# Products of b and k with the decayed rows over 64 rows, two heads side by side, and a new order of TensorE's pieces

## The chip, the cores and the metric

The kernel runs on one core of a Trainium2 chip. The metric is the device time of one execution in microseconds, median of several runs. A core has TensorE (PE in the profile: matmuls; PEld: its weight loads), VectorE (DVE), ScalarE (ACT), GpSimd (POOL) and SyncE (SP, which issues most of the DMAs here). Each engine works through its own queue in order and waits on semaphores.

## The reference, cut to what matters

Two layers of a transformer trunk for 512 latent and 128 context tokens. Each layer has three groups of heads side by side: windowed attention, full attention, and a recurrent mixer (RWKV-7 time mixing) with 6 heads of 64, run in both directions over the tokens. Only the mixer is touched. It is this scan, for each head and direction:

```
def wkv_step(S, inp):
    r, w, k, v, a, b = inp
    sa = jnp.einsum('bhvk,bhk->bhv', S, a)
    S = S * w[:, :, None, :] + sa[..., None] * b[:, :, None, :] + v[..., None] * k[:, :, None, :]
    y = jnp.einsum('bhvk,bhk->bhv', S, r)
    return S, y
...
xs = tuple(jnp.moveaxis(t, 1, 0) for t in (rh, heads(decay), kt, vh, -kk, kk * ah))
S_fin, y = lax.scan(wkv_step, init_state[:, d].astype(f32), xs, reverse=(d == 1))
```

## The kernel before, in words

All arithmetic here is in fp32, for which TensorE issues two matmul instructions for one product; the counts below are instructions as the profile shows them.

The mixer works on tiles of 128 tokens in five groups; a group is a pair of tiles, one for each direction d (the list `groups` pairs tile 0 with 3, 1 with 2, the context tile 4 with itself, 2 with 1, 3 with 0). A tile has two chunks cc of 64 tokens. The 6 heads lie as three pairs pr; in a pair, head e = 0 has partitions 0 to 63 and head e = 1 partitions 64 to 127 (`HS[e]`). A group goes through these generators:

- `front(g)`, L1039, in 15 pieces. For each direction: decay and gate projections (L1045, L1048); tanh (L1050, the one after it on VectorE L1051); the triangle sum of the log decays (L1063); exponentials; then the rows of b and k (buffer `BK`) divided by the running decay, and `W`, which holds the rows of a (columns 0 to 63) and r (64 to 127) times the running decay. `W[HS[e], e]` is written by GpSimd and VectorE (L1083, L1084); the other half, `W[HS[1-e], e]`, is cleared by GpSimd (L1082). After that, for each direction, chunk and head, the products of `BK` with `W` (L1102): four pieces for a direction, each of three products of 128 rows by 128 columns into one bank of PSUM, in which the cleared half of `W` cuts out the other head's rows. Each result is drained from PSUM by one copy on ScalarE (L1105) and two masked operations on VectorE (L1106, L1109); L1109 writes the half of `W` that was cleared. Then come 24 matmuls L1119, after which the triangles go to DRAM, and `relay(g)`. The last two pieces transpose `BK` (L1135) into `TK`: six transposes for a head into one bank, copied by ScalarE (L1137).
- `relay(g)`, L1142: 16-by-16 diagonal blocks come back from DRAM and GpSimd inverts them in 30 small operations (L1150, L1152). VectorE makes a transposed copy (L1154), and both go to DRAM again (L1156).
- `solve(g)`, L1159: loads these blocks (L1164) and inverts the whole triangles in four iterations for both directions (24 matmuls L1172 each, then VectorE L1183 or L1193).
- `rec(g)`, L1286: the recurrent steps of four chunks, each in three pieces (L1216 and L1219; L1226; L1234 and L1237), chained over the state.

Beside them run `fm_tail` (the last input projections), `bonus` and `finalize` (normalisation of the mixer's output), `tail_memory` (loads of the output weights) and `out_part` (the output projection, L1439).

The order of TensorE's instructions is written by hand: inside `tc.manual_schedule(engines={PE})` (L1442) `weave` takes one piece after another from these generators, in the order of the letters of `WEAVE` (L39): a, b, g, j, m are the fronts of groups 0 to 4; d, f, i, l, o their solves; e, h, k, n, p their recs; c the value and state transposes; q `fm_tail`; r `tail_memory`; s, t, u output projection; v to y bonus and finalize. The order on the other engines is made by the framework at compile time. The pieces of `front`, of `bonus` and of `finalize` share a ring of two PSUM banks, `pf` (L953); `BK` has two slots, `W` six, the exponentials one (`PeR`).

Of the kernel before, what the change touches and what calls it, by code (L numbers as in the profile page):

```python
# [35 lines left out]
TYPS, HELD = (1, 0), 3  # L36
MODW, BES = 512, 1
TS = (0, 1, 2, 3, 4), (0, 1, 2, 3, 4)
WEAVE = ("aqqaaqaqaqqaqqqaaqqaqaqqqaqaaqqqqqqqqqcacbbabccccbbcbccdbbbddbcbbcdbdbdgdcdbdggeggeegfgfgeggfggefgeeeeeeefggffjjjhffijjhjjjhjjhhiijhjhihhhjhhjmmjikimiimimkmklmmkklmmlmkmmlkkkklkkllnrmllmnvvnnorronovnnonnwvnnvnoorrpvrowowoppwpwsswssspwpswspwpsppswppwttwttxttwtsyutxttuuytxuttttuuuyuuuuuuuu",  # L39
         "aqqaaqaqaqqaqqqaaqqaqaqqqaqaaqqqqqqqqqcacbbabccccbbcbccdbbbddbcbbcdbdbdgdcdbdggeggeegfgfgeggfggefgeeeeeeefggffjjjhffijjhjjjhjjhhiijhjhihhhjhhjmmjikimiimimkmklmmkklmmlmkmmlkkkklkkllnrmllmnvvnnorronovnnonnwvnnvnoorrpvrowowoppwpwsswssspwpswspwpsppswppwttwttxttwtsyutxttuuytxuttttuuuyuuuuuuuu")  # L40

C_ID, C_TRI, C_MK, C_MO, C_MEAN, C_CEN, C_CS, C_AM = 0, 128, 388, 644, 772, 900, 1028, 1284
C_N = 1540
# [167 lines left out]
def trunk_kernel(ctx, tc, I, O, dbg=None, depth=DEPTH):  # L211
    nc = tc.nc
# [16 lines left out]
    ident = ct[:, C_ID:C_ID + 128]  # L229
# [325 lines left out]
    for l in range(depth):  # L555
        if True:
# [111 lines left out]
            for grp in TYPS:  # L668
                for t in ORDER:
                    p = acc()  # L670
# [280 lines left out]
            HS = (slice(0, 64), slice(64, 128))  # L951
# [12 lines left out]
            def v3(p, o=0, w=64):  # L964
                return p[:, o:o + 3 * w].rearrange("p (q t) -> p q t", q=3)
# [73 lines left out]
            def front(g):  # L1039
                for d in range(2):  # L1040
                    t = groups[g][d]
                    tk = slice(128 * t, 128 * t + 128)
                    un = unit[g, d] = {}
                    pw = pf()
                    nc.tensor.matmul(out=pw[:, :384], lhsT=tw[0:65, tk], rhs=wup[0:65, d], start=True, stop=True)  # L1045
                    pa_ = pf()
                    for pr in range(3):
                        nc.tensor.matmul(out=pa_[:, 128 * pr:128 * pr + 128], lhsT=aup[:, d, 128 * pr:128 * pr + 128], rhs=xa[:, tk], start=True, stop=True)  # L1048
                    th = thS.take()
                    nc.scalar.activation(out=th, in_=pw[:, :384], func=AF.Tanh, scale=0.5)  # L1050
                    nc.vector.tensor_scalar(out=th, in0=th, scalar1=1.0, scalar2=None, op0=ALU.add)  # L1051
                    BK = un["BK"] = BKS.take()
                    ch = lambda x: x.rearrange("p q (c j) -> p q c j", c=2)
                    tha = BK[:, :, :, 2] if t in seen else ch(THS[:, :, tk])
                    for pr in range(3):
                        nc.scalar.activation(out=tha[:, pr], in_=pa_[:, 128 * pr:128 * pr + 128].rearrange("p (c j) -> p c j", c=2), func=AF.Tanh, scale=0.5,
                                             bias=a0h[:, 6 * l + 3 * d + pr:6 * l + 3 * d + pr + 1])
                    yield

                    pc = pf()  # L1060
                    pcv = pc[:, :390].rearrange("p (q c j) -> p q c j", q=3, c=2)
                    for pr in range(3):
                        nc.tensor.matmul(out=pc[:, 130 * pr:130 * pr + 130], lhsT=th[:, 128 * pr:128 * pr + 128], rhs=tri[d], start=True, stop=True)  # L1063
                    thS.give(th)
                    Pe = PeR()[:, 0:390].rearrange("p (q c j) -> p q c j", q=3, c=2)
                    iP = iPR()
                    i0, e0 = (1, 0) if d == 0 else (0, 1)
                    nc.scalar.activation(out=Pe, in_=pcv, func=AF.Exp, scale=-CDEC)
                    nc.scalar.activation(out=iP, in_=pcv[:, :, :, i0:i0 + 64], func=AF.Exp, scale=CDEC)
                    for pr in range(3):  # L1070
                        nc.scalar.activation(out=BK[:, pr, :, 1], in_=tha[:, pr], func=AF.Identity, scale=col1(c2, pr), bias=col1(c1, pr))
                    if t in seen:
                        nc.gpsimd.tensor_tensor(out=ch(THS[:, :, tk]), in0=ch(THS[:, :, tk]), in1=tha, op=ALU.add)
                    seen.add(t)
                    made.add(("a", t, d))
                    nc.vector.scalar_tensor_tensor(out=BK[:, :, :, 0], in0=tha, scalar=1.0, in1=ch(kkh[:, :, tk]), op0=ALU.add, op1=ALU.mult)
                    nc.vector.tensor_tensor(out=BK[:, :, :, 1], in0=BK[:, :, :, 1], in1=ch(ckT[:, :, tk]), op=ALU.mult)
                    un["Wn"], W = WS["v"].popleft()
                    un["W"] = W
                    PC = un["PC"] = PCS.take()  # L1080
                    for e in range(2):
                        nc.gpsimd.memset(W[HS[1 - e], e], 0.0)  # L1082
                        nc.gpsimd.tensor_tensor(out=W[HS[e], e, :, :, 64:128], in0=ch(rT[HS[e], :, tk]), in1=Pe[HS[e], :, :, i0:i0 + 64], op=ALU.mult)  # L1083
                        nc.vector.tensor_tensor(out=W[HS[e], e, :, :, 0:64], in0=ch(kkh[HS[e], :, tk]), in1=Pe[HS[e], :, :, e0:e0 + 64], op=ALU.mult)  # L1084
                    nc.vector.scalar_tensor_tensor(out=BK[:, :, :, 0], in0=BK[:, :, :, 0], scalar=-0.5, in1=iP, op0=ALU.mult, op1=ALU.mult)
                    nc.vector.tensor_tensor(out=BK[:, :, :, 1], in0=BK[:, :, :, 1], in1=iP, op=ALU.mult)
                    nc.scalar.copy(out=BK[:, :, :, 2], in_=BK[:, :, :, 0])
                    jc = 64 if d == 0 else 0
                    nc.gpsimd.tensor_copy(out=PC, in_=Pe[:, :, :, jc:jc + 1])
                    yield  # L1090
                for d in range(2):
                    un = unit[g, d]
                    W, BK = un["W"], un["BK"]
                    un["GBn"], GB = GBS["v"].popleft()
                    un["GB"] = GB
                    for cc in range(2):

                        for e in range(2):
                            p = pf()
                            pv = v3(p, w=128)  # L1100
                            for pr in range(3):
                                nc.tensor.matmul(out=pv[:, pr], lhsT=BK[:, pr, cc, e:e + 2].rearrange("p a j -> p (a j)"), rhs=W[:, e, pr, cc],  # L1102
                                                 start=True, stop=True)

                            nc.scalar.copy(out=GB[HS[e], cc, :, 0:64], in_=pv[HS[e], :, 0:64])  # L1105
                            nc.vector.tensor_tensor(out=GB[HS[e], cc, :, 64:128], in0=pv[HS[e], :, 64:128],  # L1106
                                                    in1=mK[d][HS[e], 64:128].unsqueeze(1).to_broadcast([64, 3, 64]), op=ALU.mult)
                            o = HS[1 - e]
                            nc.vector.tensor_tensor(out=W[o, e, :, cc], in0=pv[o], in1=mK[d][o].unsqueeze(1).to_broadcast([64, 3, 128]), op=ALU.mult)  # L1109
                            yield  # L1110
# [16 lines left out]
                for d in range(2):  # L1127
                    un = unit[g, d]
                    un["TKn"], TK = B["TK"].popleft()
                    BK = un["BK"]  # L1130
                    for e in range(2):
                        p = pf()
                        for cc in range(2):
                            for pr in range(3):
                                nc.tensor.transpose(out=p[:, 192 * cc + 64 * pr:192 * cc + 64 * pr + 64],  # L1135
                                                    in_=BK[HS[e], pr, cc, e:e + 2].rearrange("p a j -> p (a j)"), identity=ident[HS[e], HS[e]])
                        nc.scalar.copy(out=TK[:, :, e], in_=p[:, :384].rearrange("p (c q t) -> p c q t", c=2, q=3))  # L1137
                    un["TK"], un["TKt"] = [TK[:, 0], TK[:, 1]], TK
                    BKS.give(BK)
                    yield  # L1140
# [289 lines left out]
            def out_part(t, k0, k1):  # L1430
                tk = slice(128 * t, 128 * t + 128)
                assert k0 or acci[t] not in held
                held.add(acci[t])
                for k in range(k0, k1):
                    assert k < 5 or ("f", t) in made
                    whi, wlo = ow[k // 2]
                    mhi, mlo = B["m"]
                    for q, (a, w) in enumerate(((mhi, whi), (mhi, wlo), (mlo, whi))):
                        nc.tensor.matmul(out=accb[t], lhsT=a[k][:, tk], rhs=w[:, k % 2, :], start=(k == 0 and q == 0), stop=(k == KD - 1 and q == 2))  # L1439
                    yield  # L1440
# [171 lines left out]
```

## Time and profile before

| | |
|---|---|
| time, median of 3 runs (lowest, highest) | 2196.01 us (2194.43, 2198.79) |
| the profiled execution: its time, its span | 2200.6 us, 2198.8 us |
| mean granted TensorE clock | 0.958 |
| TensorE busy | 1986.7 us (90% of the span), 16220 matmuls |
| VectorE / ScalarE / GpSimd busy | 1207.9 / 829.2 / 374.5 us |

The span is the time from the first to the last instruction of the profiled execution; the granted clock is the share of TensorE's full clock that the throttle granted. In the page's slices of 55 us, TensorE's busy share is 9 tenths or more nearly everywhere, with dips to 6 to 8 tenths in slices 7 to 10 and 28 to 31, the recurrent mixer of layer 0 (about 289 to 620 us) and of layer 1 (about 1354 to 1685 us).

Rows of a timeline below read: start (us from the span's start), duration (us), engine, line, operation, tiles written and read, partitions by elements, count; in brackets, how long the engine sat idle before it, and which engine's which line ended that. A tile's letter (F, H, M, ...) is the memory zone. Neighbours of the same line are merged into one row.

### The profile page before, as it was taken

To read this page: it belongs to the slowest core of one execution; us is meant where nothing else is said; L and a number is where in the kernel's file an instruction comes from. 1 tells how busy PE (TensorE), PEld (TensorE's weight loads), DVE (VectorE), ACT (ScalarE), POOL (GpSimd) and SP (SyncE) were. 2 spreads that over 40 slices of the span, in tenths; PEclk is the share of its full clock that TensorE was granted. 3 is DMA by queue.
4 is the path that set the end of the run, shared out by engine and by line. 5 is a ranking of instruction groups with operands and counts; after the bars stand their busy time and mean duration, and the time that the engine had idled before them with its cause. 6 is when DMAs were issued, how large, how long until landed. Compare 5 with 4: busy or idle time off the path is not lost. (4 is left out here: it accounts for less than half of the span.)

```text
span 2198.8 us, 39737 instructions
## 1 busy us (share of the span) xinstructions
PE 1986.7 (90%) x16220; PEld 1746.2 (79%) x16220; DVE 1207.9 (55%) x2369; ACT 829.2 (38%) x1827; POOL 374.5 (17%) x674
## 2 busy tenths in 40 slices
PE   4989998776989999999999899967779999999997
PEld 1766788665779989989977778856667899998996
DVE  1756654664778555566367785457657632222334
ACT  2645643342354222212245674444324622221221
POOL 0210013363013112121022000244420100000002
PEclk8999998888999999999999999989989999999999
DMA  8265212214226444454222002032242222222221
GB/s 271 82 196 162 67 33 33 36 33 77 85 89 183 132 135 135 125 153 128 80 83 91 12 1 68 14 50 33 48 123 82 83 72 77 77 73 77 82 68 48
DMA packets 280766, 192.14 MB, mean 87 GB/s; under 512 B 107316, under 2 KB 249614, under 8 KB 280584
## 3 DMA queue, kind: packets, MB, share of 16 engines
q1 hardware_dynamic: 259152, 139.41, 23.3%
q0 software_dynamic: 8800, 29.17, 4.5%
q10 hardware_dynamic: 12632, 21.03, 2.8%
q8 instruction: 127, 2.08, 0.4%
q14 instruction: 55, 0.45, 0.1%
HBM read 173.48 MB, written 16.08 MB: 86 GB/s over the span
## 5 line engine op out<-in xcount | busy, mean ns | idle before, releaser
L537 PE MATMUL psb<-H,B 128*128 128x320 f32 x2112 | 319.5, 311 | 2.9 <-DVE H L529 2.5
L537 PEld LDWEIGHTS psb<-H,B 128*128 128x128 f32 x2112 | 313.5, 189 | 7.5 <-DVE H L529 3.3
L537 PE MATMUL psb<-H,A 128*128 128x320 f32 x2016 | 304.5, 310 | 0.0
L537 PEld LDWEIGHTS psb<-H,A 128*128 128x128 f32 x2016 | 296.9, 188 | 2.2 <-issue 1.2
L365 DVE TENSOR_TENSOR B<-F,B 128x1024 fp32r<-128x1024 f32 (+1 forms) x78 | 94.0, 1206 | 142.9 <-ACT B L364 142.9
L494 POOL TENSOR_TENSOR r<-v,F 128x1 f32<-128x1 f32 (+1 forms) x50 | 41.9, 840 | 748.3 <-DVE v L492 737.4
L365 DVE TENSOR_TENSOR A<-F,A 128x1024 fp32r<-128x1024 f32 (+1 forms) x78 | 93.1, 1194 | 137.7 <-ACT A L364 137.6
L364 ACT CAST A<-F 128x1024 fp32r<-128x1024 f32 (+1 forms) x78 | 80.0, 1026 | 203.3 <-PE psb L537 94.8
L364 ACT CAST B<-F 128x1024 fp32r<-128x1024 f32 x80 | 82.8, 1037 | 189.7 <-PE psb L537 114.3
L537 PE MATMUL psb<-H,C 128*128 128x320 f32 x864 | 130.6, 309 | 0.0
L537 PEld LDWEIGHTS psb<-H,C 128*128 128x128 f32 x864 | 127.8, 188 | 0.2
L397 POOL DMA_DIRECT2D F<-in_w_mod x96 | 71.9, 749 | 329.2 <-DVE F L403 217.3
L405 DVE SCALAR_TENSOR_TENSOR F<-F 128x512 f32<-128x512 f32 x168 | 114.7, 745 | 20.4 <-DMA F<-in_w_mod 14.7
L1540 DVE TENSOR_TENSOR F<-F,psb 128x320 f32<-128x320 f32 x88 | 42.8, 486 | 122.1 <-PE psb L537 121.9
L547 PE MATMUL psb<-A,M 128*128 128x512 f32 x370 | 96.7, 390 | 0.0
L365 DVE TENSOR_TENSOR C<-F,C 128x1024 fp32r<-128x1024 f32 (+1 forms) x34 | 40.5, 1191 | 78.7 <-ACT C L364 78.7
L547 PEld LDWEIGHTS psb<-A,M 128*128 128x128 f32 x370 | 69.2, 188 | 15.4 <-issue 1.0
L831 DVE TENSOR_REDUCE mx<-psb 128x1 f32<-128x640 f32 (+3 forms) x100 | 64.4, 645 | 30.9 <-PE psb L813 26.4
L547 PE MATMUL psb<-B,M 128*128 128x512 f32 x310 | 77.6, 390 | 0.0
L1534 ACT ACTIVATE F<-psb 128x320 f32<-128x320 f32 x88 | 38.2, 434 | 97.5 <-PE psb L537 96.4
L1063 PE MATMUL psb<-F 128*128 128x130 f32 x120 | 25.0, 361 | 49.8 <-DVE F L1051 49.8
L364 ACT CAST C<-F 128x1024 fp32r<-128x1024 f32 (+1 forms) x34 | 34.7, 1021 | 91.0 <-PE psb L547 46.6
(421 smaller groups left out, 4059.9 us busy)
## 6 DMA issues: line engine op xcount, KB each, us to landing
F<-in_w_gu SPq DMA_DIRECT2D x88, 512.0 KB
F<-in_w_mod POOLq DMA_DIRECT2D x96, 256.0 KB, 3.5
F<-in_w_in SPq DMA_DIRECT2D x40, 512.0 KB
F<-in_w_down SPq DMA_DIRECT2D x40, 512.0 KB
F<-in_w_mod SPq DMA_DIRECT2D x38, 512.0 KB
M<-in_w_mod SPq DMA_DIRECT2D x10, 512.0 KB
F<-in_w_out SPq DMA_DIRECT2D x40, 128.0 KB
F<-in_x_sample ACTq DMA_DIRECT2D x8, 512.0 KB
```

The costliest lines, as they stand in the source:

```text
L364: nc.scalar.copy(out=hi[:, :n], in_=rawt[:, :n])
L365: (eng or nc.vector).tensor_tensor(out=lo[:, :n], in0=rawt[:, :n], in1=hi[:, :n], op=ALU.subtract)
L397: dma.dma_start(out=rv, in_=w[:, :, c0:c0 + n])
L405: nc.vector.scalar_tensor_tensor(out=ac[s][:, cc], in0=r[:, cc], scalar=sT[:, k, s:s + 1], in1=ac[s][:, cc], op0=ALU.mult, op1=ALU.add)
L494: nc.gpsimd.tensor_tensor(out=r, in0=v, in1=mhalf.to_broadcast(shape), op=ALU.pow)
L537: nc.tensor.matmul(out=ps2[hf][:, :HALF], lhsT=w[:, k, :], rhs=a[k][:, tk], start=(k == 0 and q == 0), stop=(k == KD - 1 and q == 2))
L547: nc.tensor.matmul(out=ps5[t], lhsT=a[k][:, tk], rhs=w[:, kk, :], start=(first and kk == 0 and q == 0), stop=(last and kk == nk - 1 and q ...
L831: nc.vector.reduce_max(out=mx, in_=self.S, axis=AX.XY if self.nb == 5 else AX.X)
L1063: nc.tensor.matmul(out=pc[:, 130 * pr:130 * pr + 130], lhsT=th[:, 128 * pr:128 * pr + 128], rhs=tri[d], start=True, stop=True)
L1534: nc.scalar.activation(out=sgt[:, HALF * hf:HALF * hf + HALF], in_=pg[hf][:, :HALF], func=AF.Silu)
L1540: nc.vector.tensor_tensor(out=sgt[:, tk], in0=sgt[:, tk], in1=pu[hf][:, :HALF], op=ALU.mult)
```

## The change

- The products of `BK` with `W` are taken over the 64 rows of a head instead of 128, so that the half of `W` that was cleared isn't read, and the two clearing memsets for a direction go (40 in the program).
- For a direction and chunk, the products of both heads, alternating between them, come in one piece into two banks of `pf`; the drains follow, head 0 first. The number of pieces stays: the second of the two is left without work for TensorE.
- The transposes of `BK` alternate between the heads in the same way.
- `WEAVE` is written anew for both layers, with the same number of each letter. The first 39 letters are the same. Among the differences: of group 2's solve (i), the first three iterations' pieces that stood ahead of group 3's L1119 (the 13th j) stand behind it; seven of the last eight pieces of rec 3 (n) that stood behind the first matmuls of solve 4 (the second o) stand ahead of them; four value pieces (the third to sixth c) stand behind, no longer ahead of, the fourth piece of front 1.
- An assertion on the order of the output projection is added; it makes no instruction.

```diff
@@ -36,8 +36,8 @@
-WEAVE = ("aqqaaqaqaqqaqqqaaqqaqaqqqaqaaqqqqqqqqqcacbbabccccbbcbccdbbbddbcbbcdbdbdgdcdbdggeggeegfgfgeggfggefgeeeeeeefggffjjjhffijjhjjjhjjhhiijhjhihhhjhhjmmjikimiimimkmklmmkklmmlmkmmlkkkklkkllnrmllmnvvnnorronovnnonnwvnnvnoorrpvrowowoppwpwsswssspwpswspwpsppswppwttwttxttwtsyutxttuuytxuttttuuuyuuuuuuuu",
...
+WEAVE = ("aqqaaqaqaqqaqqqaaqqaqaqqqaqaaqqqqqqqqqccababbbbbccccbbcddcbdbcdcbbdcbdbgdcbddgeggegegeggffggegefgfgeeeeeehfgffgjjjjjjhffjihhhhjhjhhhjjhjjhjmmijikiiiimiimmkkmmmlkkmmmmkmkklklkllkklrlnnllnnmvonmnvnnrnrnvnonoovvvoorwwpooropprwwwsspwsssswpspswswppppwuppwttwtxstwuuyttxttyuuyxtutututttuutuuuuu",
...
@@ -1079,7 +1079,6 @@
                     for e in range(2):
-                        nc.gpsimd.memset(W[HS[1 - e], e], 0.0)
                         nc.gpsimd.tensor_tensor(out=W[HS[e], e, :, :, 64:128], in0=ch(rT[HS[e], :, tk]), in1=Pe[HS[e], :, :, i0:i0 + 64], op=ALU.mult)
...
@@ -1095,12 +1094,13 @@
                     for cc in range(2):
 
+                        pv2 = [v3(pf(), w=128) for e in range(2)]
+                        for pr in range(3):
+                            for e in range(2):
+                                nc.tensor.matmul(out=pv2[e][:, pr], lhsT=BK[HS[e], pr, cc, e:e + 2].rearrange("p a j -> p (a j)"), rhs=W[HS[e], e, pr, cc],
+                                                 start=True, stop=True)
                         for e in range(2):
-                            p = pf()
-                            pv = v3(p, w=128)
-                            for pr in range(3):
-                                nc.tensor.matmul(out=pv[:, pr], lhsT=BK[:, pr, cc, e:e + 2].rearrange("p a j -> p (a j)"), rhs=W[:, e, pr, cc],
-                                                 start=True, stop=True)
+                            pv = pv2[e]
...
@@ -1128,12 +1128,14 @@
+                    p2 = [pf(), pf()]
+                    for cc in range(2):
+                        for pr in range(3):
+                            for e in range(2):
+                                nc.tensor.transpose(out=p2[e][:, 192 * cc + 64 * pr:192 * cc + 64 * pr + 64],
+                                                    in_=BK[HS[e], pr, cc, e:e + 2].rearrange("p a j -> p (a j)"), identity=ident[HS[e], HS[e]])
                     for e in range(2):
-                        p = pf()
-                        for cc in range(2):
-                            for pr in range(3):
-                                nc.tensor.transpose(out=p[:, 192 * cc + 64 * pr:192 * cc + 64 * pr + 64],
-                                                    in_=BK[HS[e], pr, cc, e:e + 2].rearrange("p a j -> p (a j)"), identity=ident[HS[e], HS[e]])
+                        p = p2[e]
                         nc.scalar.copy(out=TK[:, :, e], in_=p[:, :384].rearrange("p (c q t) -> p c q t", c=2, q=3))
```

## Rows read from the trace of the kernel before

**Rows 1.** Stretches of layer 0: length, busy time (instructions) by engine, clock, DMA.
```profile
347.00:373.10 26.10, 21.44 (x207) 19.07 (x206) 8.01 (x20) 11.74 (x31) 15.79 (x41) 0.87 0.08 12
373.10:390.10 17.00, 15.19 (x188) 13.51 (x190) 14.55 (x32) 5.84 (x18) 2.95 (x5) 0.80 0.47 78
390.10:414.20 24.10, 14.52 (x230) 12.42 (x226) 10.42 (x19) 8.45 (x24) 12.00 (x36) 0.81 0.19 28
414.20:430.80 16.60, 14.59 (x198) 13.11 (x200) 13.89 (x30) 7.20 (x20) 3.83 (x4) 0.87 0.36 57
430.80:456.00 25.20, 17.51 (x364) 14.74 (x360) 13.23 (x27) 9.26 (x26) 17.94 (x44) 0.94 0.16 22
456.00:477.40 21.40, 19.15 (x296) 17.41 (x298) 19.72 (x42) 10.22 (x31) 9.41 (x11) 0.84 0.29 48
477.40:496.30 18.90, 12.74 (x244) 10.71 (x240) 10.00 (x20) 10.64 (x30) 13.90 (x30) 0.93 0.14 28
496.30:519.70 23.40, 18.25 (x223) 16.36 (x223) 16.99 (x36) 5.76 (x17) 9.13 (x21) 0.76 0.36 74
519.70:547.40 27.70, 15.81 (x411) 13.88 (x410) 8.79 (x22) 5.88 (x17) 8.70 (x32) 0.89 0.40 68
547.40:620.40 73.00, 67.67 (x795) 56.17 (x796) 55.27 (x84) 29.10 (x54) 4.13 (x7) 0.95 0.33 101
```

**Rows 2.** Timeline of POOL, relay 0: start, duration, instruction, idle before.
```profile
360.51 0.73 POOL L1082 MEMSET H<- 64x768 f32 x1
...
370.58 0.73 POOL L1082 MEMSET A<- 64x768 f32 x1
...
372.19 0.22 POOL L1152 TENSOR_TENSOR F<-F,N 96x15 f32<-96x15 f32 x1
```

**Rows 3.** Timeline of DVE: first drains of the stretches, two drains, a relay's copy.
```profile
378.64 0.34 DVE L1106 TENSOR_TENSOR H<-psb,F 64x192 f32<-64x192 f32 x1
...
420.69 0.56 DVE L1109 TENSOR_TENSOR A<-psb,F 64x384 f32<-64x384 f32 x1
...
422.77 0.34 DVE L1106 TENSOR_TENSOR A<-psb,F 64x192 f32<-64x192 f32 x1
...
462.14 0.34 DVE L1106 TENSOR_TENSOR M<-psb,F 64x192 f32<-64x192 f32 x1
...
507.19 0.34 DVE L1106 TENSOR_TENSOR H<-psb,F 64x192 f32<-64x192 f32 x1
...
538.62 0.37 DVE L1154 COPY N<-F 96x256 f32<-96x256 f32 x1 [7.05 <-POOL F L1152]
```

**Rows 4.** Timeline of PE: products, transposes, the second triangle sum, changes of shape.
```profile
334.73 1.50 PE L1102 MATMUL psb<-M,F 128*128 128x128 f32 x12
335.98 2.59 PE L936 MATMUL psb<-H,B 128*128 128x320 f32 x16
...
362.38 0.58 PE L1135 MATMUL psb<-F 64*128 64x64 f32 x6
...
373.14 0.94 PE L1063 MATMUL psb<-F 128*128 128x130 f32 x6 [2.91 <-DVE F L1051]
...
421.39 0.91 PE L1102 MATMUL psb<-A,F 128*128 128x128 f32 x6 [1.38 <-ACT F L1307]
...
429.21 0.57 PE L1234 MATMUL psb<-H 128*64 128x64 f32 x12
429.71 0.56 PE L1237 MATMUL psb<-M,H 64*64 64x64 f32 x12
430.10 0.87 PE L1172 MATMUL psb<-N,M 64*64 64x64 f32 x24
...
533.99 0.77 PE L1135 MATMUL psb<-F 64*128 64x64 f32 x12
```

**Rows 5.** Timeline of PE: the two long stalls in the last group.
```profile
539.51 1.12 PE L1226 MATMUL psb<-H,B 64*64 64x64 f32 x24 [3.07 <-DVE B L1193]
...
547.45 0.47 PE L1172 MATMUL psb<-N,H 64*64 64x64 f32 x2 [6.82 <-DMA N<-dW]
```

More of the change, by code (lines that the diff above doesn't have):

```diff
@@ L38 @@
 TS = (0, 1, 2, 3, 4), (0, 1, 2, 3, 4)
-WEAVE = ("aqqaaqaqaqqaqqqaaqqaqaqqqaqaaqqqqqqqqqcacbbabccccbbcbccdbbbddbcbbcdbdbdgdcdbdggeggeegfgfgeggfggefgeeeeeeefggffjjjhffijjhjjjhjjhhiijhjhihhhjhhjmmjikimiimimkmklmmkklmmlmkmmlkkkklkkllnrmllmnvvnnorronovnnonnwvnnvnoorrpvrowowoppwpwsswssspwpswspwpsppswppwttwttxttwtsyutxttuuytxuttttuuuyuuuuuuuu",
-         "aqqaaqaqaqqaqqqaaqqaqaqqqaqaaqqqqqqqqqcacbbabccccbbcbccdbbbddbcbbcdbdbdgdcdbdggeggeegfgfgeggfggefgeeeeeeefggffjjjhffijjhjjjhjjhhiijhjhihhhjhhjmmjikimiimimkmklmmkklmmlmkmmlkkkklkkllnrmllmnvvnnorronovnnonnwvnnvnoorrpvrowowoppwpwsswssspwpswspwpsppswppwttwttxttwtsyutxttuuytxuttttuuuyuuuuuuuu")
+WEAVE = ("aqqaaqaqaqqaqqqaaqqaqaqqqaqaaqqqqqqqqqccababbbbbccccbbcddcbdbcdcbbdcbdbgdcbddgeggegegeggffggegefgfgeeeeeehfgffgjjjjjjhffjihhhhjhjhhhjjhjjhjmmijikiiiimiimmkkmmmlkkmmmmkmkklklkllkklrlnnllnnmvonmnvnnrnrnvnonoovvvoorwwpooropprwwwsspwsssswpspswswppppwuppwttwtxstwuuyttxttyuuyxtutututttuutuuuuu",
+         "aqqaaqaqaqqaqqqaaqqaqaqqqaqaaqqqqqqqqqccababbbbbccccbbcddcbdbcdcbbdcbdbgdcbddgeggegegeggffggegefgfgeeeeeehfgffgjjjjjjhffjihhhhjhjhhhjjhjjhjmmijikiiiimiimmkkmmmlkkmmmmkmkklklkllkklrlnnllnnmvonmnvnnrnrnvnonoovvvoorwwpooropprwwwsspwsssswpspswswppppwuppwttwtxstwuuyttxttyuuyxtutututttuutuuuuu")
 C_ID, C_TRI, C_MK, C_MO, C_MEAN, C_CEN, C_CS, C_AM = 0, 128, 388, 644, 772, 900, 1028, 1284
@@ L1435, in out_part @@
                     assert k < 5 or ("f", t) in made
+                    assert k == 0 or ("o", t, k - 1) in made
+                    made.add(("o", t, k))
                     whi, wlo = ow[k // 2]
```

## Prediction, made before the change was measured

> **What bounds the kernel now.** I read the page's first part and its slices first (TensorE is the busiest engine, and full nearly everywhere except in two dips, one per layer), then a table of stretches over the first dip [rows 1], then, in each stretch, the rows of TensorE, VectorE and GpSimd. The dip is the recurrent mixer, the only place that the change touches. The stretches are cut at two events. One is a group's *hand-off*: the 24 matmuls of L1119, after which the group's triangle goes through DRAM to GpSimd (relay, 30 small operations) and back. The other is the *second triangle sum* of the next group: L1063 for its direction 1. They alternate: hand-off at 347.0, second sum at 373.1, hand-off at 390.1, and so on to the fifth hand-off at 519.7. Then come relay and solve of the last group (first matmul at 547.4) and a full tail to 620.4 [rows 1].
>
> Reading: from hand-off to second sum (26.1, 24.1, 25.2, 18.9 us) TensorE is idle for 4.7 to 9.6 us and at the end stands still for VectorE's L1051, as in the row at 373.14 [rows 1, 4]. VectorE takes L1051 behind L1154, the copy that waits for the relay, as the copy at 538.62 does, or behind work that the relay holds up on GpSimd; there it is the relay, not TensorE, that ends last. From second sum to hand-off (17.0, 16.6, 21.4, 23.4 us) TensorE is 86% busy (67.2 of 78.4 us), and here lie the products of b and k with the decayed rows (L1102), which the change alters. The tail is 93% busy (67.7 of 73.0) [rows 1].
>
> **Step 1, the products and transposes.** For a direction and chunk, two pieces of six matmuls of 128 rows become one piece of twelve matmuls of 64 rows, head 0 in rows 0 to 63 and head 1 in rows 64 to 127, alternating. Twelve in a row now last 1.50 us, six 0.91: 0.1 us for each more [rows 4]. If the halves run fully side by side, twelve take what six take, 0.91; if not at all, 1.50. The row nearest is L1135: six transposes of 64 rows by 128 columns 0.58, but twelve, where the two heads' halves could meet, 0.77; one after another they would take about 1.0 [rows 4]. L1237, whose heads alternate over rows, does twelve in 0.56 [rows 4]. I take 0.91: 0.6 us less TensorE time for each of 20 pairs in a layer.
>
> A change of shape costs TensorE something: from L1234 (128 rows by 64 columns) to L1237 (64 by 64) it is 0.50 us, from L1237 to L1172 of the same shape 0.39, for twelve matmuls each [rows 4]. So 0.1 at each change; I bound it by 0 and 0.2. [...]
>
> In the first group the pairs stand between 128-row matmuls of fm_tail, and TensorE has no gaps: a pair now takes 1.25 from start to start (334.73 to 335.98) [rows 4]; then 0.91 less the 0.25 that the next overlaps (1.50 against 1.25), plus two changes: 0.86. Four pairs save 1.6; the third pair follows the second by only two pieces, so I allow 0.5 for a wait for banks: **-1.1 us** (0 to -1.6).
>
> The transposes save at most 0.2 a unit. Most lie in the shadow of a relay, so I put them at nothing (0 to -1 a layer).
>
> **Step 2, the clearing of W that goes.** 20 memsets a layer. Eight stand inside the first relay, between its 30 operations (the first at 360.51, the last at 370.58, 0.73 each), and delay its end to 372.4 [rows 2]. Without them it ends 8 x 0.73 = 5.8 us earlier. The second sum at 373.14 waited for just that [rows 4]. Will something else be late? In the new order the four value pieces that stood before this sum come behind it, so TensorE is there in time; the tanh of direction 1 could hold it. I take -5.2 (-5.8 to -2). The other twelve stand where GpSimd waits for DRAM: nothing.
>
> **Step 3, the banks.** The ring for these pieces has two banks (L953). Before, head 0 was drained from one while TensorE filled the other. Now a piece fills both, and the next piece waits until VectorE has drained both. Rows: TensorE starts at 421.39 and VectorE's first drain L1106 at 422.77, 1.4 later, ScalarE's copy between; a drain is 0.35 + 0.56 = 0.9 (L1106, L1109), two 1.8; and the next piece starts 0.14 after the end of the last drain (420.69 + 0.56 = 421.25) [rows 3, 4]. So a pair needs 1.4 + 1.8 + 0.15 = 3.4 us. From a stretch's first drain to the hand-off: 1.8 + 0.15, two periods of 3.4, and 2.4 until L1119 has head 0's bank back: **11.2 us at least**. Before: 378.64 to 390.1, 11.4; 420.33 (0.36 before L1109's row) to 430.8, 10.5; 462.14 to 477.4, 15.2; 507.19 to 519.7, 12.5 [rows 1, 3]. So where one would hope for 4 x 0.6 us a stretch, the drains give most of it back. VectorE's work for solves and steps falls partly into the pauses; I add 0.2 to 1.5: 11.4, 11.5, 12.7, 11.8, that is 0, **+1.0, -2.5, -0.7** us. The third stretch gains most since the new order moves three solve pieces (24 matmuls, 0.87 each) behind its hand-off. Bounds for each: -4 (the first drain itself earlier, as it now comes 5.5 to 10.9 us after the second sum) to +3.
>
> The waits from hand-off to second sum stay: TensorE isn't what ends them. Shorter pieces there become longer idle time.
>
> **Step 4, the tail.** Before, rec 3 stands still for 3.07 us at 539.51, until VectorE has passed the relay's copy (538.62), does its first two pieces, and then solve 4 blocks TensorE for 6.8 us at 547.45, waiting for the last relay's DMA [rows 3, 5]. In the new order seven further step pieces of rec 3 come before solve 4. Five have 24 matmuls (0.89: 429.21 to 430.10), two have 12 (about 0.5): 5.5 us [rows 4]. They fill the gap; rec 3's chain starts where it does now, 19.8 us after the hand-off, and may outlast the gap by 1 us. Behind 547.45 TensorE is idle for another 5.3 us (73.0 - 67.7) [rows 1], partly between these very pieces, where a step waits for the one before; I let 2.0 of it go with them. Tail: 1 - 5.5 - 2.0 = **-6.5** (-12 to 0).
>
> **Sum.** A layer: -1.1 - 5.2 + 0 + 1.0 - 2.5 - 0.7 - 6.5 = -15.0; both layers, whose rows agree within 1 us, -30. The profiled execution took 2200.6 us (span 2198.8), so it would take 2170.6; the median of before was 2196.0, so the median after is **2166**.
>
> **Rivals.**
> *The drains rule (slower).* One mechanism: the two-bank period in VectorE's queue. Each 1 us on the period of 3.4 costs three periods x four groups = 12 us a layer; beyond 1.25 us, a period of 4.65, the layer is slower than before. At a period of 5.0: -15 + 19 = +4 a layer, 2204. For it: the eight drains of a group took 10.5 to 15.2 us before, so VectorE's other work and waits made 0.4 to 1.0 us of each, 0.8 to 2.0 of a pair. Against it: a period has a pause of 1.4 + 0.15 in which VectorE can do just that work. [...] 9%.
> *The halves don't run side by side (the change doesn't do what it says).* 0.6 on each period and on the first group's pairs: 12 x 0.6 + 4 x 0.6 = 9.6 a layer lost of 15: 2185. The 0.77 of L1135 speaks against it. 7%.
> *The tail gives nothing.* VectorE could take the relay's copy ahead of solve 3's last additions, so that rec 3 comes later still: -8.5 a layer, 2179. 20%.
> *More is freed.* The first drains of three stretches come 4 us earlier, because VectorE takes them ahead of the next direction's products: -27 a layer, 2142. 14%.
>
> **How the numbers follow.** Forecast 50%. The range 2138 to 2192 leaves out the slower rival and little of the last. Within 0.2% (4.4 us, about what a measurement can tell) lies only the edge between the drains' rival and the others: 0.05; slower 0.08; faster 0.87.
>
> **What would show it.** L1102 as twelve matmuls of 64 rows in 0.9 us (1.5: the second rival). The first relay's last operation and the second sum behind it 5 to 6 us closer to their hand-off. First drain to hand-off 11 to 13 us in each group (above 15: the first rival), with TensorE's idle time before L1102 put down to L1109. No long stall of TensorE at solve 4's first matmul. It would be wrong if VectorE's order differs much from now: the order on the other engines isn't written out, and rests on no row.

## The result, and the profile after

The changed kernel takes 2174.1 us (median, 2171.4 to 2176.6), the kernel before 2197.4 beside it: ratio 0.990, 95% interval 0.9883 to 0.9916, some 23 us faster. Forecast were 2166 and a gain of 30. The profiled execution took 2174.8 us (span 2172.8).

Layer 0 after, cut at the same events as [rows 1]; columns: length, busy time (instructions) of TensorE, its weight loads, VectorE, ScalarE and GpSimd, granted clock (1.00 is called the higher level below and 0.50, the lowest that any of these stretches shows, the lower), DMA share, GB/s.

```profile
344.25:368.85 24.60, 19.01 (x158) 16.60 (x158) 8.09 (x19) 9.29 (x25) 11.32 (x35) 0.81 0.27 43
368.85:386.65 17.80, 14.93 (x259) 12.92 (x259) 14.35 (x32) 7.13 (x24) 2.82 (x3) 0.78 0.20 33
386.65:409.82 23.17, 12.24 (x202) 10.37 (x202) 8.85 (x18) 8.40 (x23) 11.08 (x34) 0.87 0.19 27
409.82:429.46 19.64, 17.07 (x224) 15.19 (x225) 14.83 (x32) 8.02 (x25) 6.62 (x9) 0.63 0.32 51
429.46:453.38 23.92, 14.33 (x293) 11.84 (x289) 12.59 (x25) 9.00 (x26) 13.72 (x38) 0.89 0.17 23
453.38:473.56 20.18, 18.77 (x295) 16.23 (x295) 17.96 (x40) 10.55 (x31) 7.52 (x8) 0.79 0.25 51
473.56:497.03 23.47, 17.94 (x311) 15.28 (x311) 13.44 (x27) 10.19 (x28) 16.24 (x40) 0.78 0.12 17
497.03:514.16 17.13, 11.60 (x154) 9.60 (x152) 13.84 (x30) 6.41 (x19) 4.67 (x7) 0.87 0.56 108
514.16:545.70 31.54, 24.96 (x606) 22.32 (x606) 13.54 (x34) 6.85 (x20) 10.73 (x35) 0.91 0.42 74
545.70:606.58 60.88, 58.01 (x657) 48.05 (x654) 52.88 (x77) 30.20 (x57) 3.12 (x5) 1.00 0.38 115
```

Against [rows 1]: fifth hand-off to end 92.4 us, was 100.7; first to fifth hand-off 169.9, was 172.7. In layer 1 the same two are 91.0 (was 100.4) and 176.0 (was 171.8): there the groups got *slower*. So most of the gain lies behind the last hand-off, not in the stretches that hold the products. The second row to look at is the fourth: second sum to hand-off, 19.64 where it was 16.6, at a granted clock of 0.63 where it was 0.87.

Three timelines round the first relay (start, duration, line, idle before). GpSimd's last operation of the relay, answering [rows 2]:

```profile
361.90 0.22 POOL L1154 TENSOR_TENSOR F<-F,N 96x15 f32<-96x15 f32 x1
```

VectorE behind it, first before, then after:

```profile
360.61 0.85 DVE L1051 TENSOR_SCALAR F<-F 128x384 f32<-128x384 f32 x1 [0.46 <-ACT F L1050]
...
372.45 0.37 DVE L1154 COPY N<-F 96x256 f32<-96x256 f32 x1 [6.53 <-POOL F L1152]
372.74 0.35 DVE L1051 TENSOR_SCALAR F<-F 128x384 f32<-128x384 f32 x1
```

```profile
362.16 0.37 DVE L1156 COPY N<-F 96x256 f32<-96x256 f32 x1 [5.58 <-POOL F L1154]
362.45 0.35 DVE L1051 TENSOR_SCALAR F<-F 128x384 f32<-128x384 f32 x1
...
368.45 0.35 DVE L1051 TENSOR_SCALAR F<-F 128x384 f32<-128x384 f32 x1
```

TensorE: the second sum, a product piece at the higher clock, solve 4's first piece; answering [rows 4, 5]:

```profile
368.85 1.67 PE L1063 MATMUL psb<-F 128*128 128x130 f32 x6 [1.66 <-DVE F L1051]
...
468.25 0.94 PE L1100 MATMUL psb<-M,F 64*128 64x128 f32 x12
...
545.70 0.87 PE L1174 MATMUL psb<-N,H 64*64 64x64 f32 x24
```

The relay ends 17.9 us after its hand-off, where it was 25.4. But VectorE's copy behind it (L1154 before, L1156 after), which waits for it, now stands ahead of direction 0's L1051 too, and direction 0's whole chain ahead of direction 1's. So the second sum comes 6.7 us after the relay's end, where it was 0.7, and only 1.5 us nearer to its hand-off. The twelve matmuls take 0.94 us, and solve 4 starts without a stall.

### The profile page after: what moved, and what is told of

Read it like the earlier page. It is cut to its first block, busy times and chain, and to the rows that moved or that the text cites. A ratio compares the mean times of both kernels' runs of the same rounds, so it can differ in the third digit from the quotient of the medians.

```text
span 2172.8 us, 39707 instructions
## 1 busy us (share of the span) xinstructions
PE 1972.3 (91%) x16220; PEld 1727.2 (79%) x16220; DVE 1205.6 (55%) x2369; ACT 829.4 (38%) x1827; POOL 348.6 (16%) x634
## 5 line engine op out<-in xcount | busy, mean ns | idle before, releaser
L547 PEld LDWEIGHTS psb<-B,M 128*128 128x128 f32 x310 | 58.0, 188 | 12.8 <-issue 0.8
```

Of the source, the lines that this page charges most:

```text
L547: nc.tensor.matmul(out=ps5[t], lhsT=a[k][:, tk], rhs=w[:, kk, :], start=(first and kk == 0 and q == 0), stop=(last and kk == nk - 1 and q ...
```

## The experiments

### Order, products and clearing apart

Ratios are to the kernel before, measured beside each run (2196 to 2198 us), with 95% intervals; products over 64 rows are "in turn" (head after head, in separate pieces) or "side by side", and with side by side go the paired transposes. A letter (theory A, rival B, ...) is that of the expectation in which it stands.

| kernel | order | products | clearing | us | ratio |
|---|---|---|---|---|---|
| before | old | 128 rows | yes | 2197 | 1 |
| e8 | old | 64, in turn | yes | 2222.4 | 1.0120 (1.0103 to 1.0137) |
| e3 | old | 64, in turn | no | 2224.1 | 1.0122 (1.0100 to 1.0143) |
| e2 | old | 64, side by side | no | 2227.1 | 1.0131 (1.0112 to 1.0150) |
| e1 | new | 128 rows | yes | 2167.0 | 0.9863 (0.9843 to 0.9883) |
| e7 | new | 64, side by side | yes | 2189.4 | 0.9967 (0.9954 to 0.9979) |
| after | new | 64, side by side | no | 2174.1 | 0.9900 (0.9883 to 0.9916) |

**The new order alone** (e1): the two lines of WEAVE from the change, nothing else.

> The kernel before with the new order of TensorE's pieces alone; products over 128 rows with the clearing, heads in separate pieces' loops as before. Theory A (the gain of the change is the new order after the fourth hand-off, 8.3 and 9.4 us per layer, and the removal of the clearing was given back): 2178 to 2182 us, 16 to 20 us under the kernel before, with the last hand-off to the end of the weave at 91 to 93 us in layer 0 (100.7 before). Rival B (the gain comes from the shorter products and the removed clearing; the order only fits them): within 5 us of the kernel before.

Measured: 31 us under before, more than the whole change gives. That is theory A, and beyond its 16 to 20. The tail gives 8.4 and 8.2 us in the two layers (92.3 and 92.2 from the fifth hand-off to the end), and from first to fifth hand-off another 7.0 and 7.1.

**Products and clearing in the old order** (e2): the changed kernel with the old WEAVE.

> The changed kernel with the order of pieces of the kernel before: 64-row products side by side, paired transposes, no clearing. Theory A: 0 to 6 us under the kernel before: the first relay is about 7 us shorter, but VectorE's copy behind it now stands ahead of the scaling for the second sum, so the sum follows the relay's end by about 6 us and the wait from hand-off to sum is cut by 1 to 2 us only. Rival B: 15 to 23 us under, as the whole change. Rival C (the removal of the clearing pays as it was forecast): 10 us under, 5 per layer, with the wait from the first hand-off to the second sum at 21 us.

All three expectations missed: it is 29 us *slower* than before.

**No clearing** (e3), and **64 rows with the clearing kept** (e8). e8 has only the first of these two edits, e3 both:

```
-  lhsT=BK[:, pr, cc, e:e + 2]..., rhs=W[:, e, pr, cc],
+  lhsT=BK[HS[e], pr, cc, e:e + 2]..., rhs=W[HS[e], e, pr, cc],
...
-  nc.gpsimd.memset(W[HS[1 - e], e], 0.0)
```

> The kernel before with one edit: products over 64 rows, head after head as they stand, and so no clearing; pieces and order of TensorE as before. Theory A (the copy behind the relay comes to stand ahead of the second sum's scaling on VectorE): 0 to 4 us under the kernel before; first relay 10 to 11 us long (18.0 before), second sum 6 us after its end. Rival C (the forecast): 10 us under, wait of 21 us from hand-off to second sum.

> The kernel before with one edit: the products read 64 rows instead of 128, heads in turn as they stand; the clearing stays, though nothing reads what it clears, and the orders of all engines stay as they are. Against the run with the clearing removed as well (2224 us) it parts the two causes in the old order. Theory E (64 rows, lower clock in the product stretches): 10 to 20 us over the kernel before, granted clock in 400 to 500 us below 0.82 (0.86 before). Rival F (VectorE's order alone makes the loss of 26 us): within 4 us of the kernel before.

e3 is 26 us slower, against both expectations. e8 says why, above theory E's range: with the order of every engine left as it was, reading 64 rows instead of 128 alone costs 26 us; dropping the clearing then changes nothing that can be told (the intervals overlap). The relay is 7.5 us shorter in e3, but there too the copy moves ahead, and in layer 0 L1051 for the second sum starts 25.0 us after the hand-off against 25.7 in e8. The sum itself, behind value pieces (L1017) on TensorE, comes at 28.2 against 26.1.

**The changed kernel with the clearing kept** (e7): the memset line put back.

> The changed kernel with the clearing put back on GpSimd, though nothing reads the cleared halves: products over 64 rows side by side, new order. Against the run of the new order alone (2167 us, products over 128 rows) it differs by the products and the paired transposes only. Theory E (the product stretches run at the lower level of TensorE's clock for longer when the products are over 64 rows, mean granted clock in 400 to 500 us 0.79 in the changed kernel against 0.88 with the new order alone): 5 to 20 us over the new order alone, product stretches of layer 1 at 52 us or more in sum against 44.7, granted clock in 400 to 500 us below 0.83; removing the clearing then was worth about 0 to 5 us in the changed kernel. Rival F (the shorter products cost nothing, all of the loss is in VectorE's order that comes with the removed clearing): within 3 us of 2167 us, granted clock at 0.88.

Theory E, slightly above its range: 22 us over the new order alone, granted clock 0.80 from 400 to 500 us. Unlike e8, e7 has other orders of VectorE, ScalarE and GpSimd than the run that it is compared with, since the compiler made them anew, so its 22 us isn't the products' alone for certain. And the changed kernel is 15 us under e7, where 0 to 5 were expected: in the new order the clearing's end did pay. The two kernels have the same order on TensorE, and on VectorE it differs by the place of one copy in each layer; 3.3 and 3.7 of the 15 us lie in the two layers' waits before group 1's first drain and 3.3 in the stretches of layer 0 (53.0 to 49.7); where the rest lies is open. So the change parts into -31 (order), +22 (64-row products) and -15 (no clearing). These steps lead from one kernel to the other, so that their sum, -24 against -23 measured, tests only the noise; taken in another order the steps have other sizes, as e8 and e3 show.

Most of the 22 and 26 us is seen from first drain (L1106, the first copy of a product out of PSUM on VectorE) to hand-off in groups 1 to 4, counted from 0: 18 us between the profiled executions of e1 and e7, which lie 26 us apart, and 19 between those of before and e8, which lie 28 apart, both layers together. The stretches of layer 1 before:

```profile
1445.47:1455.92 10.45, 8.42 (x133) 7.48 (x134) 9.07 (x23) 3.90 (x13) 0.00 (x0) 1.00 0.38 58
1485.63:1497.09 11.46, 10.30 (x145) 9.27 (x146) 9.78 (x25) 3.20 (x10) 0.99 (x1) 0.85 0.10 19
1528.42:1542.95 14.53, 12.90 (x252) 11.62 (x254) 13.87 (x34) 5.16 (x17) 4.84 (x7) 1.00 0.17 26
1572.76:1585.00 12.24, 11.18 (x145) 10.11 (x145) 9.76 (x26) 2.53 (x9) 0.62 (x2) 0.74 0.40 93
```

64 rows in the old order (e8):

```profile
1461.88:1474.98 13.10, 12.81 (x152) 11.57 (x150) 9.24 (x23) 4.00 (x13) 0.00 (x0) 0.65 0.29 53
1504.98:1520.15 15.17, 15.12 (x149) 13.48 (x150) 10.08 (x25) 3.90 (x12) 1.50 (x2) 0.50 0.08 14
1552.45:1569.71 17.26, 16.39 (x254) 14.78 (x255) 14.28 (x34) 5.17 (x17) 5.40 (x7) 0.69 0.14 22
1599.55:1612.24 12.69, 11.33 (x144) 10.18 (x144) 9.76 (x26) 2.54 (x9) 0.61 (x2) 0.68 0.40 90
```

New order, 128 rows (e1):

```profile
1427.98:1438.32 10.34, 10.20 (x222) 9.31 (x220) 9.99 (x28) 4.93 (x16) 0.00 (x0) 1.00 0.22 39
1466.58:1477.87 11.29, 10.46 (x172) 9.10 (x173) 10.96 (x29) 4.66 (x14) 2.18 (x3) 1.00 0.11 19
1507.59:1521.21 13.62, 13.07 (x241) 11.38 (x235) 12.58 (x34) 5.75 (x18) 5.97 (x8) 1.00 0.44 75
1550.01:1559.46 9.45, 7.40 (x96) 6.51 (x98) 8.58 (x24) 2.87 (x10) 0.93 (x1) 1.00 0.51 117
```

New order, 64 rows, clearing kept (e7):

```profile
1442.08:1454.52 12.44, 10.52 (x192) 9.36 (x193) 9.98 (x26) 4.73 (x17) 0.00 (x0) 0.73 0.11 22
1483.13:1497.97 14.84, 13.12 (x156) 11.85 (x158) 11.45 (x30) 3.98 (x13) 2.18 (x3) 0.55 0.08 14
1528.98:1542.24 13.26, 11.81 (x238) 9.93 (x235) 12.43 (x34) 5.22 (x17) 5.02 (x7) 1.00 0.42 77
1571.30:1585.04 13.74, 9.47 (x97) 7.88 (x98) 9.04 (x24) 3.51 (x12) 0.93 (x1) 0.70 0.33 68
```

The changed kernel:

```profile
1426.45:1438.78 12.33, 10.72 (x193) 9.46 (x193) 9.98 (x26) 4.73 (x17) 0.00 (x0) 0.67 0.12 22
1467.75:1482.52 14.77, 13.35 (x156) 11.98 (x158) 11.38 (x30) 3.97 (x13) 2.17 (x3) 0.54 0.08 14
1513.24:1526.51 13.27, 11.75 (x239) 9.88 (x233) 12.44 (x34) 5.22 (x17) 2.09 (x3) 1.00 0.41 77
1555.57:1570.04 14.47, 10.72 (x97) 8.88 (x98) 9.04 (x24) 3.50 (x12) 0.93 (x1) 0.57 0.25 62
```

The column to read is the clock, third from the end. The sums of the lengths are 48.7, 58.2, 44.7, 54.3 and 54.8 us, and in either order a stretch is longer where its clock has fallen. In the third rows of the new order, all at 1.00, 64 rows take no longer than 128 (13.62, 13.26 and 13.27 us). In e8's second row TensorE is busy 15.12 of 15.17 us at 0.50: it has become the bound. Its pieces there, in the timeline of TensorE (start, duration):

```profile
1511.47 2.30 PE L1102 MATMUL psb<-A,F 64*128 64x128 f32 x12
1513.70 1.54 PE L1172 MATMUL psb<-N,H 64*64 64x64 f32 x24
1515.17 2.24 PE L1102 MATMUL psb<-A,F 64*128 64x128 f32 x12
```

and the same three before, at 1.00 (0.70 from the start of their stretch to the first of them):

```profile
1491.25 1.94 PE L1102 MATMUL psb<-A,F 128*128 128x128 f32 x12
1493.11 0.91 PE L1172 MATMUL psb<-N,H 64*64 64x64 f32 x24
1493.96 1.60 PE L1102 MATMUL psb<-A,F 128*128 128x128 f32 x12
```

The solve piece between is the same in both kernels and takes 1.54 instead of 0.91: in these stretches it is above all the lower level, which all pieces share, that makes the loss. A smaller part of the 26 us is not the clock's. In group 0, at 1.00 throughout in both kernels, e8 needs 23.63 us from second sum to hand-off where before needed 21.45: 2.2 us a layer, 4.4 of the 26. There the products stand in seven places between 128-row matmuls, so at 14 changes of shape it would be some 0.16 us each (an estimate; no run parts it from the rest of the edit, nor tells what it adds in groups 1 to 4).

### VectorE's copy

**The copy on GpSimd** (e4, from the changed kernel):

```
-  nc.vector.tensor_copy(out=VT, in_=V.rearrange("p s t -> p t s"))
+  nc.gpsimd.tensor_copy(out=VT, in_=V.rearrange("p s t -> p t s"))
```

> The changed kernel with one edit: the copy that follows each relay goes from VectorE to GpSimd, so that VectorE never stands waiting for a relay; the rest of VectorE's order stays. Theory A (VectorE held at the copy is what gave the shorter relay back and what lengthened the fourth wait): the second sum comes 3 to 6 us nearer to its hand-off, the fourth wait falls from 23.5 to 19 or 20 us, 10 to 30 us under the changed kernel in all. Rival D (the copy costs GpSimd as much as VectorE's wait did, its products for the next direction come later by the same): within 4 us of the changed kernel.

2166.8 us (0.9856, 0.9833 to 0.9878): 7 us under the changed kernel, between the two theories. In layer 0 the second sums of groups 1 to 3 come 3.6, 6.6 and 6.6 us nearer to their hand-offs, so VectorE's place for the copy did hold them. But the first drains come only 1.8, 2.2 and 0.9 us nearer: behind the sums TensorE's first products wait 0.7, 2.1 and 4.7 us for GpSimd's products of the rows (L1082), which stand after the relay and now after the copy too. The fourth wait did not fall (24.2): TensorE stands without idle time before that sum, so there its own new order sets the time.

**All of it together** (e10): the new order, 128 rows, the memset of W on VectorE, the copy on GpSimd.

> A version meant to beat both: new order, products over 128 rows as before, the clearing on VectorE instead of GpSimd and the copy behind the relay on GpSimd instead of VectorE. Theory E and A together: the first relay is 10 to 12 us long, VectorE never stands at a copy, so the wait from the first hand-off to the second sum falls from 27 to 20 to 22 us, and the granted clock in the product stretches stays at 0.88: 5 to 15 us under the new order alone, 2152 to 2162 us. Rival G (VectorE's own work, longer by twenty clearings a layer, or GpSimd's later products take the room): within 4 us of 2167 us.

2167.2 us (0.9863, 0.9849 to 0.9877): rival G, no better than the new order alone. Hand-offs to first drains are 6 us shorter in sum (115 against 121), but the stretches 4 us longer (48.6 against 44.7, the second and fourth at 0.73 and 0.84 of the clock). From the first hand-off to the end the layers are 4.8 and 3.6 us shorter, yet stretches outside, where the kernels are alike, are 4.0 and 3.7 us longer; why is open. e1, e4 and e10 can't be told apart; each beats both kernels.

### The heads in turn

e6: the changed kernel, the two loops over heads and pairs exchanged.

```
-  for pr in range(3):
-      for e in range(2):
+  for e in range(2):
+      for pr in range(3):
```

> The changed kernel with the twelve matmuls of a product piece in another order: per piece the three of head 0 and then the three of head 1, so that neighbours use the same 64 rows instead of the other 64. If running side by side pays on the path: 0.6 us more per piece, 40 pieces, 10 to 20 us over the changed kernel. If the two banks and their drains set the pace, as was predicted: within 4 us of it, though the piece itself takes 1.5 us instead of 0.94.

2185.6 us (0.9957, 0.9943 to 0.9970), 11.5 over the changed kernel, as if side by side paid. But the profiled execution is the quickest of its six (2174.4; the others 2184 to 2191), so its trace doesn't show the 11.5. It shows a piece at the higher clock

```profile
468.06 1.26 PE L1100 MATMUL psb<-M,F 64*128 64x128 f32 x12
```

at 1.26 us against 0.94, and the stretch round it 13.27 us long against 13.26 in the changed kernel. So here the longer piece does not lengthen the stretch; the other runs' lower mean clock (0.942 to 0.949, the changed kernel's 0.953) goes with their time. VectorE's order differs in places too; what part each has stays open.

### Can the clock be held up?

**More work over all rows** (e12, from e8): ahead of each product

```
+  nc.tensor.matmul(out=pv[:, pr], lhsT=ident, rhs=ct[:, 128 * pr:128 * pr + 128], start=True, stop=True)
```

> The kernel with 64-row products in the old order and the clearing kept (2222 us), with work added: ahead of each three products over 64 rows, three matmuls over all 128 rows of constants (identity times a table, 128x128) go into the same bank and are overwritten. That is 480 matmuls a run more, some 130 us of TensorE time at 0.27 us each. Theory E (what the 64-row products lose is the granted clock, and more activity over all rows brings it back): mean granted clock in 400 to 500 us at 0.84 or more (0.76 without the added work, 0.86 before), and the time in spite of the added work at or under 2222 us, 2195 to 2222. Rival H (the loss has to do with 64-row operands as such, their loads or their landing in the banks): the added work comes on top, 2230 to 2270 us.

2430 us, 207 over e8: theory E's cure failed, and by more than rival H allowed. The 480 added records (240 matmuls of two) last 0.42 us in the median, so all of their time is on the path. Layer 0, first two stretches:

```profile
395.99:433.55 37.56, 37.56 (x209) 27.67 (x208) 9.98 (x23) 4.60 (x14) 0.00 (x0) 0.50 0.10 15
463.25:502.06 38.81, 38.81 (x226) 28.67 (x224) 10.93 (x27) 4.62 (x14) 1.58 (x2) 0.50 0.03 5
```

and TensorE inside the second:

```profile
465.81 0.79 PE L1103 MATMUL psb<-A,F 64*128 64x128 f32 x2
466.54 0.79 PE L1102 MATMUL psb<-F 128*128 128x128 f32 x2
467.26 0.79 PE L1103 MATMUL psb<-A,F 64*128 64x128 f32 x2
```

TensorE never pauses for 37 us and stays at the lower level, though every other matmul is over all 128 rows. And two records start every 0.72 us, where twelve 64-row ones took 2.30 at the same level, 0.38 for two: what is left, some 0.3 us for each two, would by estimate from these two rows be the change of shape that my edit had put at every matmul; no run adds such matmuls without it.

**Work ahead of the products** (e14, from the changed kernel; e13, the same from e10; e15, from e1, ahead of the second sum): eight matmuls (e15: 6, 4, 5, 3) of

```
+  nc.tensor.matmul(out=p2[0][:, :512], lhsT=ident, rhs=ct[:, 0:512], start=True, stop=True)
```

> The changed kernel with the same added work: eight matmuls of constants (128x512) before the first product piece of groups 1 to 4. Theory E: product stretches of layer 1, 54.8 us in sum in the changed kernel, fall to 46 to 50 us, total 2162 to 2172 us; if the clock falls again within the stretch because the 64-row products don't hold it, stretches stay at 53 us or more and the total within 4 us of 2174 us.

2204.8 us (1.0034, 1.0021 to 1.0046). The total missed; the stretches of layer 1, 49.0 us in sum, lie in the expected 46 to 50. Layer 0, second and fourth:

```profile
428.96:440.28 11.32, 8.61 (x173) 7.30 (x170) 9.38 (x23) 3.36 (x11) 1.19 (x2) 1.00 0.11 20
...
521.78:532.39 10.61, 8.15 (x126) 6.67 (x122) 8.06 (x20) 3.35 (x11) 0.00 (x0) 0.91 0.19 51
```

They take 13.4 and 12.3 us in the changed kernel, at 0.62 and 0.82. So with 64-row products a stretch can be at 1.00 from first drain to hand-off and as short as e1's (11.3). It need not: in layer 1 the same two are 14.0 us at 0.63 and 11.1 at 0.84. And the added matmuls came behind the sum, not in idle time: first drains came 17 to 18 us a layer later.

> The version with new order, 128-row products, clearing on VectorE and the copy on GpSimd (2167 us), with work added: before the first product of groups 1 to 4 eight matmuls of constants (128x512) into the bank that this product then overwrites, 0.5 to 0.8 us each, in the idle stretch before the products. If the product stretches are slow because TensorE enters them at the lower level: product stretches of layer 1 in sum 44 to 46 us against 48.6, total 2155 to 2163 us. If the lower level in these stretches costs nothing on the path: within 3 us of 2167 us; if the matmuls come too late and delay the products: 2172 us or more.

> The new order alone (2167 us) with work added in TensorE's idle time: 6, 4, 5 and 3 matmuls of constants (128x512, 1.2 us each at the higher level) into the bank of the second sum of groups 1 to 4, ahead of that sum, which waits 9.0, 5.9, 7.9 and 4.7 us for VectorE's scaling there. In the new order alone that sum runs at the lower level (1.67 us against 0.94) and so does the first product piece (1.5 against 0.9). If the clock is held by the added work: 1.0 to 1.4 us less per group, eight groups, 2156 to 2160 us. If the sum's time isn't on the path (the drains' operands come later anyway) or the clock falls again before the sum: within 3 us of 2167 us.

2200.6 (1.0014, 1.0005 to 1.0023) and 2192.4 us (0.9978, 0.9969 to 0.9988): 33 and 25 slower than without the added work. The added records of e13, two for a matmul, last 0.59 us in the median and 1.22 at most. In e13 it again came too late, its waits from hand-off to first drain 13 to 15 us a layer longer, and the stretches of layer 1 (49.7 us) were no shorter than e10's 48.6. In e15 it lay in idle time, but 3.7 us of it were left ahead of group 1's second sum in layer 0, which still took 1.67 us at 0.50. The waits grew by 7 and 9 us, nearly all of it between second sum and first drain, and two stretches of each layer fell to 0.73 to 0.84 of the clock where e1 has 1.00. The order of the other engines changed with it (the compiler sets it anew), so e15 doesn't separate the two.

## Why the prediction was right and wrong

The time lay in the range and the sign was right, 8 us from the forecast. That closeness is in part luck, since errors of either sign offset each other: the tail gave more than forecast, the products' stretches took where they should have given, and 8 us of the difference between the profiled executions lie where no step looked.

- *Step 1.* The halves do run side by side: 0.94 us for twelve (0.91 forecast; 1.26 in turn, e6), first group, from second sum to hand-off, -0.94 us in both layers (-1.1 forecast). What failed is the price of 64 rows on the whole: taken as a gain, it is +22 us by e7 against e1, +26 in the old order.
- *Step 2.* The relay became 7.5 us shorter (5.8 forecast). Of the -5.2 for the second sum 1.5 came, as VectorE's order put the copy first, and at the first drain nothing was left of it (in layer 0 31.6 us after the hand-off, before and after). VectorE's order was the one condition that the text named as resting on no row. Against e7, that is within one order of TensorE, the wait to the first drain fell by 3.3 and 3.7 us, inside the bounds of -5.8 to -2.
- *Step 3.* This is the step that failed. The two-bank period held where the clock was high: in group 1 of layer 0, at 0.97, the pieces behind the first drain start 3.0 and 3.4 us apart, and the stretch of 10.8 us came out just under the floor of 11.2. But against 11.4, 11.5, 12.7 and 11.8 us forecast, the four stretches took 10.8, 13.4, 13.3 and 12.3, in layer 1 12.3, 14.8, 13.3 and 14.5. The sum, forecast -2.2 a layer, was +0.1 and +6.2. The missing term is the granted clock: [rows 1] had 0.76 to 0.87 round these stretches, and the sum used durations at either level without asking which level the changed work would get. In the second stretch of layer 0 TensorE is busy without a gap from 420 to 428 us, nearly all of it at 0.50; a piece takes 2.11 us instead of 0.94, the first drain comes 2.1 us after its start (1.4 in the sum), and the next piece 3.7 after it. So there TensorE at the lower level sets the pace, not the drains. In e1, all at 1.00, the sum is -4.9 and -4.0.
- *The waits.* Beyond the -5.2 of step 2 they were put at 0; from hand-offs to first drains all four together became 2.8 and 1.9 us shorter.
- *Step 4.* Right in mechanism, too small: -6.5 forecast, -8.3 and -9.4 measured. Solve 4 starts 31.5 us after the hand-off (27.7), without its stall, and the rest is 60.9 us (73.0): +3.8 and -12.1 where +1 and -7.5 were forecast, so more moved ahead of solve 4 than the sum had. e1 has the same 8 us, so it is the order's.
- *Rivals.* "The halves don't run side by side" is out by the 0.94. "The drains rule" is not what happened: the long stretches go with the clock, and in e14's second stretch of layer 0, at 1.00, the pieces behind the first drain start 3.3 and 3.0 us apart. "The tail gives nothing" is out by the 8.3 and 9.4. "More is freed" is out too: no first drain came more than 1.5 us nearer to its hand-off. No rival named the clock.

The layers give -12.0 and -6.1 us. The other 8 us between the profiled executions lie outside these stretches; some 3 of them are that the profiled execution of before, at 2200.6, was slower than the median of 2197.4 measured beside the changed kernel.

## What to carry to other kernels

Where TensorE's work is made smaller, read the granted clock of that stretch and price the rest of the stretch at both levels: here products of half the rows, by themselves as short as forecast at the higher level (0.94 us), came with a lower level that slowed all their neighbours (e8's second stretch of layer 1 at 0.50 where before had 0.85, the same solve piece 1.54 us instead of 0.91). Test each part of a combined change alone; the new order without its products is the better kernel. And where a compiler sets the order on an engine, an operation can move ahead of a critical one when its input comes earlier: read that order again after every edit.

## What the hardware showed beyond that

With the same instructions in the same order, and products over 64 instead of 128 rows (e8 against before, layer 1), the granted clock of the stretches went from between 0.74 and 1.00 to between 0.50 and 0.69, although half of the `W` that the 128-row form read was zeros. In e8 and e12 TensorE had records almost without a pause for 15 and 37 us at 0.50 (15.12 of 15.17 us busy and 37.56 of 37.56), and no rise came. Where the level was high on entry, 64-row products did not end it at once: from second sum to hand-off of group 0 the changed kernel stays at 1.00 for 20.5 us and e8 for 23.6, there between 128-row matmuls, and e14's second stretch of layer 0 for 11.3 us; in layer 1 that one has 0.63. So in these rows a busy TensorE alone did not bring the higher level. Why the lower level holds with half-row products stays open; in e12 full-row matmuls between them did not end it (0.50 for 37.56 us), and whether its changes of shape had a part no run shows.
